# Hybrid encoder layer: modulations in steps of 256 columns with half the buffers, and S5 table products that may go to VectorE or GpSimd

## The chip, the cores and the metric

The kernel runs on one core of one Trainium2 chip, in one launch. The metric is the device time of one execution in microseconds (us). Of the kernel before three executions were timed; a fourth was profiled, and all traces here are of that one.

## What is computed

One encoder layer on x (1024 tokens by 1024 features, float32), conditioned on a vector c. Cut to what matters:

```python
mod = (silu(c) @ w_ada + b_ada).reshape(1, 3, 3, 1024)   # shift, scale, gate for three sub-layers
f1 = swiglu(modulate(x, mod[0, 0], mod[0, 1]), w_up1, w_down1)
x = layer_norm(alpha * x + (1 + mod[0, 2]) * 0.5 * f1)
tm = token_mixer(modulate(x, mod[1, 0], mod[1, 1]))      # [mLSTM heads | S5 groups], one input
x = layer_norm(alpha * x + (1 + mod[1, 2]) * tm)         # and one output projection
f2 = swiglu(modulate(x, mod[2, 0], mod[2, 1]), w_up2, w_down2)
x = layer_norm(alpha * x + (1 + mod[2, 2]) * 0.5 * f2)
```

The S5 half of the mixer is a complex diagonal recurrence over 32 groups of 64 states in two directions. Powers of its coefficients, times its input and output matrices, depend on the weights alone and can be made ahead of the tokens: the kernel calls them tables.

## The kernel before, in words

Every matrix product of tokens is done in float32 precision by splitting each operand into a rounded part and a remainder and adding three products (`mm3`, 6936 such matmuls of 128x512 in all). The splitting, two operations for each 128x512 tile, is the largest work of VectorE (DVE).

**Order of the work.** The program is straight-line code. A planner writes it: `run_jobs` goes through the matmul jobs of the main stream in a fixed order (start, first SwiGLU up, first down product, input projections, GLU, output projection in two halves, second SwiGLU), and between them `pump` takes operations out of lanes, generators such as the layer norms, the modulations and the tables (lane "bg"), the S5 mixing, the mLSTM. `Clock` keeps a planned time for each engine, with a cost for each operation, and emits an operation when its operands should be ready. `nc.any.f(...)` gives the planner the choice of VectorE or GpSimd (POOL), `nc.copy` that of ScalarE (ACT) or VectorE; `pick` takes the engine that would be done first. So every edit can move operations anywhere behind it.

**Buffers.** 99 tiles of 128x512 (`NSLOT`) are shared by all; loads of weights run ahead as far as free tiles allow. All DMAs are issued by SyncE (SP), in the order in which the planner emits them. PSUM has 8 banks.

**Modulations** (`ada`, L637 to L678). Seven of the nine modulations are made in the background during the start: for modulation j and half y (512 columns) eight tiles of `w_ada` are loaded one step ahead, 32 small matmuls against the padded vector `cpad` fill one bank, one copy takes it out, and 16 column sums per half (`fin`, `colsum`) bring it into columns.

**Tables** (`s5_gen`, L1440 to L1704). After the modulations. For each of 16 blocks two 128x320 products per table half and for each of 8 pairs of groups two 128x512 products go to GpSimd by name (`P.tensor_tensor`), each next to a VectorE product with which it is then combined; these fill the DRAM tables `Wd` and `Vd`. At the end 16 steps make the table `Ed`, each with one GpSimd product, one VectorE product, one VectorE combination and one store (L1671 to L1694).

**Who waits.** The first layer norm (`ln`) closes the first down product; the mixer's S5 part reads the tables; the output projection's second half (the passes END) needs the mLSTM of all eight chunks of tokens, each closed by `finalize` (statistics, a scaling, four transposes of 128x128, four scaled copies).

Of the kernel before, what the change touches and what calls it, by code (L numbers as in the profile page):

```python
# [11 lines left out]
OP = mybir.AluOpType  # L12
# [383 lines left out]
class Kern:  # L396
# [240 lines left out]
    def ada(self, js):  # L637


        nc = self.nc  # L640
        todo = [(j, y) for j in js for y in range(2)]

        def load(j, y):
            return [self.ada_load(j, 4 * y + x) for x in range(4)]

        nxt = load(*todo[0])
        pa = {}
        prev = None

        def fin(j, y, acc):  # L650
            for x in range(4):
                self.colsum(pa[j][:, 4 * y + x:4 * y + x + 1], acc[:, x * 128:(x + 1) * 128], self.one)
            if y:
                nc.vector.tensor_tensor(self.mods[:, j * 8:j * 8 + 8], pa[j][:, :8],
                                        self.v["b_ada"][:, j * 8:j * 8 + 8], op=OP.add)
                self.free(pa[j])

        for i, (j, y) in enumerate(todo):
            w, nxt = nxt, load(*todo[i + 1]) if i + 1 < len(todo) else None
            yield  # L660
            pb = self.bank()
            for x in range(4):
                for kc in range(KD):
                    c = slice(kc % 4 * 32, kc % 4 * 32 + 32)
                    nc.tensor.matmul(pb[c, x * 128:x * 128 + 128], self.cpad[:, kc, :], w[x][kc // 4][:, kc % 4, :],
                                     start=x == 0 and kc < 4, stop=x == 3 and kc >= 4)
            del w
            acc = self.S()
            nc.copy(acc, pb)
            yield  # L670
            if y == 0:
                pa[j] = self.bank(True)
            if prev:
                fin(*prev)
            prev = (j, y, acc)
            del acc
            yield
        fin(*prev)  # L678

    def mod(self, sub, which):  # L680
# [698 lines left out]
    def s5_gen(self):  # L1379
        nc, I = self.nc, self.I  # L1380
        V, P = nc.vector, nc.gpsimd
# [151 lines left out]
        for j in range(2, 10):  # L1533
            x, y = j // 2, j - j // 2
# [3 lines left out]
        pw = [self.S([128, G, 10]) for _ in range(2)]  # L1538
        pv_ = self.S([128, 2, G, 8])
        pv = [pv_[:, c] for c in range(2)]  # L1540
# [10 lines left out]
        for q in range(4):  # L1551
# [4 lines left out]
            br, bi_, cr, ci = (bc[:, i] for i in range(4))  # L1556
# [3 lines left out]
            cv = self.S([128, 4, 8, 16])  # L1560
            t1, t2, cv = cv[:, 2], cv[:, 3], [cv[:, c] for c in range(2)]
# [17 lines left out]
            for b4 in range(2):  # L1579
                b = 2 * q + b4  # L1580
                ws = []
                for b2_ in range(2):
                    bt = 2 * b + b2_
                    gs = slice(2 * bt, 2 * bt + 2)
                    ls_ = slice(4 * b4 + 2 * b2_, 4 * b4 + 2 * b2_ + 2)
                    w = [self.S([128, 2, 10, 16]) for _ in range(2)]
                    t1, t2 = self.S([128, 2, 10, 16]), self.S([128, 2, 10, 16])

                    def bcs(x):
                        return x[:, ls_].unsqueeze(2).to_broadcast([128, 2, 10, 16])  # L1590

                    def bcj(x):
                        return x[:, gs].unsqueeze(3).to_broadcast([128, 2, 10, 16])

                    P.tensor_tensor(t2, bcs(ci), bcj(pw[1]), op=OP.mult)
                    V.tensor_tensor(t1, bcs(cr), bcj(pw[0]), op=OP.mult)
                    yield
                    V.tensor_tensor(w[0], t1, t2, op=OP.subtract)
                    P.tensor_tensor(t2, bcs(ci), bcj(pw[0]), op=OP.mult)
                    yield  # L1600
                    V.tensor_tensor(t1, bcs(cr), bcj(pw[1]), op=OP.mult)
                    yield
                    V.scalar_tensor_tensor(w[1], t1, -1.0, t2, op0=OP.mult, op1=OP.subtract)
                    yield
                    for c in range(2):
                        nc.sync.dma_start(
                            self.Wd[b, c, :, b2_ * 256:(b2_ + 1) * 256].rearrange("p (g x) -> p g x", g=2),
                            w[c][:, :, 1:9, :].rearrange("p g j h -> p g (j h)"))
                    ws.append(w)
                    del t1, t2, w  # L1610
                    yield
                for c in range(2):
                    for gi in range(2):
                        for b2_ in range(2):
                            co = slice(32 * (2 * b4 + b2_), 32 * (2 * b4 + b2_) + 32)
                            for d in range(2):
                                l = slice(d * 64, d * 64 + 64)
                                g = 4 * b4 + 2 * b2_ + gi
                                nc.tensor.matmul(pks[d][co, :128], cz[c][l, g],
                                                 ws[b2_][c][l, gi, 2 * d:2 * d + 8].rearrange("p j h -> p (j h)"),  # L1620
                                                 start=c + gi == 0, stop=c + gi == 2)
                del ws
                yield
                gs = slice(4 * b, 4 * b + 4)
                ls_ = slice(4 * b4, 4 * b4 + 4)

                def vb(x):
                    return x[:, ls_].unsqueeze(2).to_broadcast([128, 4, 8, 16])

                def vj(x):  # L1630
                    return x[:, gs].unsqueeze(3).to_broadcast([128, 4, 8, 16])

                for c in range(2):
                    t1, t2 = self.S([128, 4, 8, 16]), self.S([128, 4, 8, 16])
                    P.tensor_tensor(t2, vb(cv[1]), vj(pv[1 - c]), op=OP.mult)
                    V.tensor_tensor(t1, vb(cv[0]), vj(pv[c]), op=OP.mult)
                    yield
                    yield
                    V.tensor_tensor(t1, t1, t2, op=OP.subtract if c == 0 else OP.add)
                    yield  # L1640
                    pt = self.bank()
                    for g in range(4):
                        nc.tensor.transpose(pt[:, g * 128:(g + 1) * 128],
                                            t1[:, g].rearrange("p j h -> p (j h)"), self.ident)
                    vt = self.S()
                    nc.scalar.activation(vt, pt, AF.Copy)
                    nc.sync.dma_start(self.Vd[b, c], vt)
                    del t1, t2, vt
                    yield
            yield  # L1650
            kc = self.S([128, 240])
# [24 lines left out]
        for b in range(8):  # L1676
            gs = slice(4 * b, 4 * b + 4)

            def A(c):
                return ea[:, c, gs].unsqueeze(3).to_broadcast([128, 4, 8, 16])  # L1680

            def B(c):
                return eb[c][:, gs].unsqueeze(2).to_broadcast([128, 4, 8, 16])

            for c in range(2):
                t1, t2 = self.S([128, 4, 8, 16]), self.S([128, 4, 8, 16])
                P.tensor_tensor(t2, A(1), B(1 - c), op=OP.mult)
                V.tensor_tensor(t1, A(0), B(c), op=OP.mult)
                yield
                yield  # L1690
                V.tensor_tensor(t1, t1, t2, op=OP.subtract if c == 0 else OP.add)
                yield
                nc.sync.dma_start(self.Ed[b, c], t1.rearrange("p g a b -> p (g a b)"))
                del t1, t2  # L1694
# [741 lines left out]
```

## Time and profile before

| | before |
|---|---|
| timed executions, us | 1943.98, 1948.27, 1949.53 (median 1948.27) |
| profiled execution, us | 1945.06 |
| its span, first to last instruction, us | 1942.9 |
| mean granted TensorE clock, share of full | 0.981 |
| PE busy, us (share of the span) | 1855.7 (96%) |
| DVE busy | 1588.7 (82%) |
| ACT busy | 650.0 (33%) |
| POOL busy | 289.5 (15%) |
| DMA, mean | 150 GB/s |

PE is TensorE, PEld its weight loads, which overlap matmuls. Matmuls are pipelined and their recorded ends modelled, so a busy PE is not one at its peak. Busy times are unions: two DVE operations that follow each other closely overlap by some hundredths of a microsecond in the records. Nearly every instruction carries the line of one helper (L79), so groups are told apart by engine, operation and shape. A tile is named by its kind: `s` one of the 99 tiles, `b` a bank, `in_...` an input.

### The profile page before, as it was taken

What the parts mean: (1) busy time and instruction counts of PE and PEld (TensorE: products, weight loads), DVE (VectorE), ACT (ScalarE), POOL (GpSimd) and SP (SyncE); (2) the same over time, 40 slices, a digit from 0 to 9 for tenths busy, and PEclk for the clock granted to TensorE, in tenths of its full rate; (3) what the DMA queues carried; (4) which work ended last, traced back from release to release, by engine and by line L of the source; (5) the groups of instructions that cost most, each with busy time, mean ns of one, the idle gap of its engine ahead of it and who ended that gap; (6) DMA issues with size and microseconds to landing.
All of it is one profiled execution on the core that took longest, in us unless ns stands there. A gap on an engine that the chain in (4) does not pass through costs nothing.

```text
span 1942.9 us, 29666 instructions
## 1 busy us (share of the span) xinstructions
PE 1855.7 (96%) x10544; PEld 1470.2 (76%) x10544; DVE 1588.7 (82%) x3267; ACT 650.0 (33%) x1190; POOL 289.5 (15%) x284
## 2 busy tenths in 40 slices
PE   5999999999999899899999899999999999999996
PEld 3677887777878677777778677678888888887775
DVE  7937889888899999879887797898677767697887
ACT  4513333333324125622243432542222222233412
POOL 0000001122100212101022421301111111100014
PEclk9999999999999999999999799999999999999998
DMA  9983233434577445575434430224233323574512
GB/s 326 361 304 137 88 129 107 136 127 133 161 276 242 155 151 194 187 214 167 149 102 129 125 105 12 76 77 136 82 113 104 109 81 109 174 259 143 183 44 76
DMA packets 187587, 290.54 MB, mean 150 GB/s; under 512 B 27280, under 2 KB 55056, under 8 KB 187440
## 3 DMA queue, kind: packets, MB, share of 16 engines
q1 hardware_dynamic: 187440, 288.65, 44.7%
q8 instruction: 83, 1.36, 0.3%
q14 instruction: 64, 0.52, 0.1%
HBM read 218.26 MB, written 70.32 MB: 149 GB/s over the span
## 4 chain that ended last, share of the span: by engine, by line
PE 76%; DVE 14%; DMA 5%; issue 3%; ACT 1%; SPq 0%; DVEq 0%; POOL 0%; ACTq 0%; POOLq 0%
PE b L79 76%; DVE s L79 13%; DMA s<-in_w_ada 1%; ACT s L79 1%; DMA s<-Wr 1%; DMA s<-in_x 1%; DVE er L79 0%; DMA s<-Vd 0%; SPq L79 0%; DMA s<-in_glu_w 0%; DMA s<-Wd 0%; DMA s<-Md 0%; DMA s<-Td 0%; DMA s<-in_w_first 0%; DVE mr L79 0%
## 5 line engine op out<-in xcount | busy, mean ns | idle before, releaser
L79 PE MATMUL b<-s 128*128 128x512 f32 (+6 forms) x9208 | 1825.6, 371 | 50.1 <-DVE s L79 34.9
L79 PEld LDWEIGHTS b<-s 128*128 128x128 f32 (+4 forms) x9208 | 1428.4, 177 | 417.5 <-DVE s L79 52.7
L79 DVE TENSOR_TENSOR s<-s 128x512 f32<-128x512 f32 (+6 forms) x1718 | 993.0, 622 | 63.7 <-ACT s L79 37.7
L79 ACT ACTIVATE s<-s 128x512 fp32r<-128x512 f32 (+2 forms) x682 | 400.9, 625 | 579.0 <-DVE s L79 379.0
L79 POOL TENSOR_TENSOR s<-s 128x512 f32<-128x512 f32 (+2 forms) x185 | 253.9, 1386 | 1190.7 <-DVE s L79 530.3
L79 DVE TENSOR_TENSOR s<-s,b 128x512 f32<-128x512 f32 (+2 forms) x332 | 209.8, 650 | 193.7 <-PE b L79 191.4
L79 ACT ACTIVATE s<-b 128x512 f32<-128x512 f32 (+2 forms) x207 | 117.4, 576 | 483.4 <-PE b L79 438.2
L79 DVE CAST s<-s 128x512 fp32r<-128x512 f32 (+1 forms) x237 | 123.2, 522 | 9.8 <-DMA s<-in_x 3.6
L79 POOL MEMSET s<- 128x4 f32 (+4 forms) x65 | 10.1, 189 | 323.5 <-DVE s L79 246.4
L79 DVE SCALAR_TENSOR_TENSOR s<-b,gcol,s 128x512 f32<-128x512 f32 x56 | 39.4, 743 | 22.1 <-PE b L79 22.1
L79 ACT ACTIVATE s<-b,vec 128x128 f32<-128x128 f32 (+3 forms) x57 | 23.6, 464 | 84.5 <-PE b L79 82.7
L79 DVE TENSOR_TENSOR_SCAN s<-s 4x128 f32<-4x128 f32 (+1 forms) x48 | 33.4, 713 | 0.4
L79 PE MATMUL b<-ident,s 128*128 128x128 f32 (+1 forms) x208 | 30.9, 278 | 0.2 <-DVE dn L79 0.2
L79 PEld LDWEIGHTS b<-ident,s 128*128 128x128 f32 (+1 forms) x208 | 24.8, 148 | 7.6 <-issue 1.9
L79 DVE SCALAR_TENSOR_TENSOR s<-s 128x320 f32<-128x320 f32 (+3 forms) x43 | 26.6, 625 | 4.4 <-ACT s L79 4.0
L79 ACT ACTIVATE s<-s,vec 128x512 f32<-128x512 f32 x26 | 19.5, 779 | 27.7 <-DVE s L79 27.7
L79 DVE SCALAR_TENSOR_TENSOR s<-s,vec 128x512 f32<-128x512 f32 (+1 forms) x36 | 26.9, 768 | 0.1
L79 ACT ACTIVATE s<-s,Bp,Gp 128x512 f32<-128x512 f32 x26 | 20.1, 805 | 18.2 <-DVE s L79 18.2
L79 ACT ACTIVATE s<-s,gcols 128x128 f32<-128x128 f32 x64 | 20.1, 393 | 5.3 <-POOL s L79 5.3
L79 PE MATMUL b<-one,s 128*32 128x1 f32 x576 | 9.4, 173 | 12.4 <-DVE s L79 12.0
L79 PEld LDWEIGHTS b<-one,s 128*32 128x32 f32 x576 | 8.4, 112 | 16.7 <-DVE s L79 12.4
L79 DVE SCALAR_TENSOR_TENSOR s<-s,gcol 128x512 f32<-128x512 f32 x24 | 18.0, 748 | 0.6
(102 smaller groups left out, 325.0 us busy)
## 6 DMA issues: line engine op xcount, KB each, us to landing
s<-in_w_up SPq DMA_DIRECT2D x170, 256.0 KB
s<-in_w_ada SPq DMA_DIRECT2D x144, 256.0 KB
Td<-s SPq DMA_DIRECT2D x140, 256.0 KB
s<-Td SPq DMA_DIRECT2D x140, 256.0 KB
s<-in_w_down SPq DMA_DIRECT2D x124, 256.0 KB
s<-in_x SPq DMA_DIRECT2D x32, 256.0 KB
Xd<-s SPq DMA_DIRECT2D x32, 256.0 KB
s<-in_w_vo SPq DMA_DIRECT2D x32, 256.0 KB
```

What stands on the lines that cost most here:

```text
L79: self.eng, self.alts, self.emit = eng, (), lambda: getattr(real, name)(*args, **kw)
```

## The change

In `ada` a step now covers 256 columns: four steps for each modulation in place of two, each with four loads in flight one step ahead in place of eight, 16 small matmuls and one copy of 128x256. Two steps share one tile `acc`, and the column sums run after every second step, as many as before. In `s5_gen` the four products that named GpSimd now go through `nc.any`: in the loops these are 32 products of 128x320 and 32 of 128x512 (16 for `Vd`, 16 for `Ed`).

```diff
-        todo = [(j, y) for j in js for y in range(2)]
+        todo = [(j, y) for j in js for y in range(4)]
 
         def load(j, y):
-            return [self.ada_load(j, 4 * y + x) for x in range(4)]
+            return [self.ada_load(j, 2 * y + x) for x in range(2)]
...
-                self.colsum(pa[j][:, 4 * y + x:4 * y + x + 1], acc[:, x * 128:(x + 1) * 128], self.one)
-            if y:
+                self.colsum(pa[j][:, 2 * y + x - 2:2 * y + x - 1], acc[:, x * 128:(x + 1) * 128], self.one)
+            if y == 3:
...
-            for x in range(4):
+            for x in range(2):
                 for kc in range(KD):
...
-            acc = self.S()
-            nc.copy(acc, pb)
+            if acc is None:
+                acc = self.S()
+            nc.copy(acc[:, y % 2 * 256:y % 2 * 256 + 256], pb[:, :256])
...
-            if prev:
-                fin(*prev)
-            prev = (j, y, acc)
-            del acc
+            if y % 2:
+                if prev:
+                    fin(*prev)
+                prev, acc = (j, y, acc), None
...
-                    P.tensor_tensor(t2, bcs(ci), bcj(pw[1]), op=OP.mult)
+                    nc.any.tensor_tensor(t2, bcs(ci), bcj(pw[1]), op=OP.mult)
...
-                    P.tensor_tensor(t2, bcs(ci), bcj(pw[0]), op=OP.mult)
+                    nc.any.tensor_tensor(t2, bcs(ci), bcj(pw[0]), op=OP.mult)
...
-                    P.tensor_tensor(t2, vb(cv[1]), vj(pv[1 - c]), op=OP.mult)
+                    nc.any.tensor_tensor(t2, vb(cv[1]), vj(pv[1 - c]), op=OP.mult)
...
-                P.tensor_tensor(t2, A(1), B(1 - c), op=OP.mult)
+                nc.any.tensor_tensor(t2, A(1), B(1 - c), op=OP.mult)
```

**Order, first place: GpSimd during the tables.** `MEMSET s 128x4x16` stands at the start of each of the four rounds of `Wd` and `Vd`; the rows of 128x320 and 128x512 between are the products. Before:

```order
L79 MEMSET s 128x4x16 x4
L79 TENSOR_TENSOR s<-s 128x320 x4
L79 TENSOR_TENSOR s<-s 128x512 x2
L79 TENSOR_TENSOR s<-s 128x320 x4
L79 TENSOR_TENSOR s<-s 128x512 x24
L79 TENSOR_SCALAR s<-s,vec 128x512 x2
```

and now:

```order
L79 MEMSET s 128x4x16 x8
L79 TENSOR_TENSOR s<-s 128x512
L79 MEMSET s 128x4x16 x8
L79 TENSOR_TENSOR s<-s 128x512 x7
L79 TENSOR_SCALAR s<-s,vec 128x512
```

No product of a table is left on GpSimd: all 32 of 128x320 and, by the counts of the whole program, 42 operations of 128x512 (32 of them the tables') have gone to VectorE.

**Order, second place: SyncE at the end of the first down product.** `s<-Td_101` is the last load of that product's left factors, `s<-in_w_f` the first weights of the mixer, `Xd<-s` the store of the first layer norm, `Ud<-s` that of the mixer's S5 input. Before:

```order
L79 DMA s<-Td_101 128x512
L79 DMA Ed<-s 128x512 x2
L79 DMA s<-in_w_f 128x512 x4
L79 DMA Ed<-s 128x512 x2
L79 DMA s<-in_w_f 128x512 x6
L79 DMA Xd<-s 128x512 x6
L79 DMA s<-in_w_f 128x512 x2
L79 DMA Xd<-s 128x512 x2
L79 DMA Ed<-s 128x512
L79 DMA Ud<-s 128x8x64
```

and now:

```order
L79 DMA s<-Td_101 128x512
L79 DMA s<-in_w_f 128x512 x6
L79 DMA Xd<-s 128x512 x6
L79 DMA s<-in_w_f 128x512 x2
L79 DMA Xd<-s 128x512
```

Nine of the sixteen stores of `Ed` stood behind `s<-Td_101` before (five here, four a few rows on); now all sixteen stand ahead of it.

**Order, third place: TensorE at the end of the mLSTM.** `b<-ident,s 128x128 x4` are the transposes of one chunk's `finalize`, `b<-s 128x512` matmuls of the main stream, `b<-s 128x129` and `b<-s 64x129` matmuls of the mLSTM. Before:

```order
L79 MATMUL b<-s 128x129 x4
L79 MATMUL b<-s 128x512 x27
L79 MATMUL b<-ident,s 128x128 x4
L79 MATMUL b<-s 128x512 x27
L79 MATMUL b<-ident,s 128x128 x4
L79 MATMUL b<-s 128x512 x9
L79 MATMUL b<-ident,s 128x128 x4
L79 MATMUL b<-s 128x512 x15
L79 MATMUL b<-ident,s 128x128 x4
L79 MATMUL b<-s 128x512 x21
L79 MATMUL b<-ident,s 128x128 x4
L79 MATMUL b<-s 128x512 x6
```

and now:

```order
L79 MATMUL b<-s 128x129 x4
L79 MATMUL b<-s 128x512 x9
L79 MATMUL b<-s 128x129 x4
L79 MATMUL b<-s 128x512 x6
L79 MATMUL b<-ident,s 128x128 x4
L79 MATMUL b<-s 128x512 x15
L79 MATMUL b<-ident,s 128x128 x24
L79 MATMUL b<-s 128x512 x132
```

The transposes of the last six chunks now follow each other with no matmul of the main stream between them, and the matmuls that stood there have moved up between those of the mLSTM.

## Rows read from the trace of the kernel before

**Rows 1.** The page, busy time of each engine and its share of the span.

```profile
PE 1855.7 (96%) x10544; PEld 1470.2 (76%) x10544; DVE 1588.7 (82%) x3267; ACT 650.0 (33%) x1190; POOL 289.5 (15%) x284
```

**Rows 2.** Stretches: busy us of each engine, granted clock, DMA share, GB/s.

```profile
50.00:100.00 50.00, 49.44 (x854) 34.24 (x853) 47.19 (x86) 26.05 (x44) 2.44 (x2) 1.00 0.99 356
302.00:537.60 235.60, 235.55 (x1210) 183.49 (x1208) 208.43 (x384) 77.89 (x140) 50.82 (x60) 1.00 0.43 139
632.50:806.00 173.50, 155.32 (x762) 122.86 (x761) 169.10 (x291) 65.13 (x109) 36.21 (x24) 0.95 0.51 169
1041.70:1222.00 180.30, 171.66 (x935) 134.62 (x934) 134.79 (x489) 66.79 (x178) 47.65 (x41) 0.92 0.29 85
```

**Rows 3.** Waits of the weight loads, 28 to 165 us.

```profile
PEld b L79 <- DMA s<-in_w_ada: 3.0, 8, 0.5
```

**Rows 4.** Groups of ScalarE by form, 17 to 302 us: copies out of a bank.

```profile
L79 ACT ACTIVATE s<-b 128x512 f32<-128x512 f32 x41 | 24.4, 598 | 98.3 <-PE b L79 98.2
```

**Rows 5.** Groups of VectorE by form, 150 to 300 us, no product on GpSimd.

```profile
L79 DVE TENSOR_TENSOR s<-s 128x512 f32<-128x512 f32 x56 | 37.2, 687 | 0.7
L79 DVE TENSOR_TENSOR s<-s 128x512 fp32r<-128x512 f32 x53 | 36.5, 689 | 10.1 <-ACT s L79 9.4
```

**Rows 6.** Groups of VectorE by form, 302 to 537.6 us.

```profile
L79 DVE TENSOR_TENSOR s<-s 128x512 f32<-128x512 f32 x101 | 73.0, 749 | 1.4
L79 DVE TENSOR_TENSOR s<-s 128x512 fp32r<-128x512 f32 x77 | 60.9, 800 | 8.0 <-ACT s L79 7.1
L79 DVE TENSOR_TENSOR s<-s,b 128x512 f32<-128x512 f32 x44 | 30.1, 684 | 16.8 <-PE b L79 16.2
L79 DVE TENSOR_TENSOR s<-s 128x320 f32<-128x320 f32 x47 | 23.7, 514 | 0.2
```

**Rows 7.** Groups of GpSimd by form, 302 to 537.6 us.

```profile
L79 POOL TENSOR_TENSOR s<-s 128x320 f32<-128x320 f32 x32 | 30.8, 967 | 160.7 <-DVE s L79 146.5 <-PE b L79 9.9 <-DMA Wd<-s 3.1
L79 POOL TENSOR_TENSOR s<-s 128x512 f32<-128x512 f32 x16 | 19.8, 1245 | 24.7 <-PE b L79 18.2 <-DVE s L79 4.0 <-DMA Td<-s 2.5
```

**Rows 8.** Groups of VectorE and GpSimd by form, 632.5 to 806 us.

```profile
L79 DVE TENSOR_TENSOR s<-s 128x512 fp32r<-128x512 f32 x100 | 70.2, 746 | 0.9 <-ACT s L79 0.3
L79 DVE TENSOR_TENSOR s<-s 128x512 f32<-128x512 f32 x74 | 52.4, 738 | 1.3 <-ACT s L79 1.1
...
L79 POOL TENSOR_TENSOR s<-s 128x512 f32<-128x512 f32 x19 | 25.5, 1355 | 84.6 <-DVE s L79 43.6 <-PE b L79 24.1 <-ACT s L79 16.8
L79 POOL TENSOR_TENSOR s<-s 128x512 fp32r<-128x512 f32 x3 | 8.4, 2803 | 28.5 <-ACT s L79 28.5
```

**Rows 9.** Waits of the weight loads, 632 to 806 us.

```profile
PEld b L79 <- DVE s L79: 20.2, 5, 8.6
```

**Rows 10.** The end of the first layer norm's wait, columns as in rows 2.

```profile
770.00:790.00 20.00, 14.03 (x51) 10.30 (x50) 19.46 (x31) 13.36 (x23) 4.29 (x4) 0.83 0.41 147
```

**Rows 11.** The DMAs that store and read the table Ed.

```profile
L79 SPq DMA_DIRECT2D Ed<-s x16: 319/320/507, 655.2 to 802.6; - x16
L79 SPq DMA_DIRECT2D s<-Ed x16: 320/387/707, 826.4 to 946.9; - x16
```

**Rows 12.** The mLSTM where no matmul of the main stream runs, columns as in rows 2.

```profile
1061.00:1118.00 57.00, 51.24 (x368) 40.07 (x366) 42.66 (x147) 26.27 (x81) 25.26 (x25) 0.79 0.42 121
```

**Rows 13.** The chain that ended last, at the end of the mLSTM (start us, us).

```profile
1162.14 24.31 issue
1186.49 1.26 POOL s L79
1187.80 12.35 PE b L79 x52
```

More of the change, by code (lines that the diff above doesn't have):

```diff
@@ L640, in ada @@
         nc = self.nc
-        todo = [(j, y) for j in js for y in range(2)]
+        todo = [(j, y) for j in js for y in range(4)]
         def load(j, y):
-            return [self.ada_load(j, 4 * y + x) for x in range(4)]
+            return [self.ada_load(j, 2 * y + x) for x in range(2)]
         nxt = load(*todo[0])
-        pa = {}
+        pa, acc = {}, None
         prev = None
@@ L665, in ada @@
                     nc.tensor.matmul(pb[c, x * 128:x * 128 + 128], self.cpad[:, kc, :], w[x][kc // 4][:, kc % 4, :],
-                                     start=x == 0 and kc < 4, stop=x == 3 and kc >= 4)
+                                     start=x == 0 and kc < 4, stop=x == 1 and kc >= 4)
             del w
-            acc = self.S()
-            nc.copy(acc, pb)
+            if acc is None:
+                acc = self.S()
+            nc.copy(acc[:, y % 2 * 256:y % 2 * 256 + 256], pb[:, :256])
             yield
```

## The prediction

> **What bounds the kernel now.** I read the page first, then the busy time of each engine by stretches of the main stream, then, where TensorE is not full, the waits and the groups by form. On the page PE is busy 96% of the span, DVE 82%, ACT 33%, POOL 15% [rows 1]. So at most 1942.9 − 1855.7 = 87 us of idle PE can be had, and only in the places where it lies. The stretches [rows 2] show where the edited code stands: at the start (50 to 100 us) PE works 49.4 of 50 us, while the DMAs are at 0.99 of their time and 356 GB/s; during the tables (302 to 537.6 us, second half of the first SwiGLU) PE works 235.55 of 235.60 us; around the first layer norm (632.5 to 806) only 155.3 of 173.5 us, with DVE at 169.1; around the mLSTM (1041.7 to 1222) 171.7 of 180.3 us at a clock of 0.92. Only the last two have time to give. In the stretch of the layer norm DVE sets the pace, and the weight loads wait 20.2 us for its tiles [rows 9].
>
> **The start.** The edit of the modulations leaves the work of PE as it was. It has half as many `w_ada` loads ahead, so ten of the first `w_up1` loads go out eight loads earlier, and the last `w_ada` load later. Eight loads of 128x512 float32 are 2.1 MB, at 356 GB/s [rows 2] 5.9 us: the most that an earlier weight could give. The other way, the weight loads waited for `w_ada` eight times, 3.0 us together [rows 3]; with half the cover I let that double, +3.0. Between −5.9 and +3.0 I take 0, since PE is full there already. The fourteen more copies out of a bank cost ACT less than 14 × 0.598 = 8.4 us [rows 4], half that for half the width, on an engine that works a third of the time: 0; without that cover they delay a column sum, not a matmul of the main stream.
>
> **Tables of 302 to 538 us.** Thirty-two products of 128x320 and sixteen of 128x512 leave POOL and come to DVE. One of 128x320 takes DVE 0.514 us [rows 6], one of 128x512 0.687 us when POOL is quiet [rows 5]: 32 × 0.514 + 16 × 0.687 = 27.4 us more work. Something comes back: with POOL's products beside them, DVE's two-input operations took 749 and 800 ns [rows 6], without them 687 and 689 [rows 5]. That is 101 × 0.062 + 77 × 0.111 = 14.8 us, so DVE has 12.6 us net to fit in. It stood idle 235.6 − 208.4 = 27.2 us there [rows 2], 16.2 of that waiting for PE [rows 6], and PE has no gap. So I take 0, with +12.6 as the upper bound if the products fall between a split and the weight load that needs it. POOL spent most of its time waiting for DVE (146.5 us [rows 7]), so a table step ends earlier when one engine does both products. The order shows this: all sixteen `Ed` stores now stand ahead of `s<-Td_101`, nine behind it before.
>
> **The first layer norm, 632 to 806 us.** Before, `Ed` steps run up to 802.6 us [rows 11], beside the layer norm, and the first reader comes at 826.4. Their early end is the gain: from 770 to 790 us DVE is busy 19.46 of 20, and PE idles 20 − 14.03 = 6.0 us at a clock of 0.83, 20 × 0.17 = 3.4 us [rows 10]. With nine steps gone I take both back: −9.4. Against that, sixteen products at 0.687 come to DVE, 11.0 us, in a stretch where it is saturated. The lengthening there is 100 × (0.746 − 0.689) + 74 × (0.738 − 0.687) = 9.5 us over 22 POOL operations [rows 5, 8]; with 16 of the 22 gone, 6.9 come back. Net +4.1, all of it on the path. Sum for the stretch −9.4 + 4.1 = −5.3. Bounds: −20.2, the whole wait [rows 9], and +11.0 if nothing comes back.
>
> **The mLSTM.** No operation is edited here, but the planner, behind a changed history, has put the main matmuls elsewhere. Before, 57 us (1061 to 1118) held no main matmul: PE idled 57 − 51.24 = 5.8 us, and at a clock of 0.79 lost 57 × 0.21 = 12.0 us [rows 12]. Now some run in between. But they are taken from the end: the transposes of the last six `finalize` follow each other with nothing between, where before the main matmuls covered them. How much they covered is seen in the chain: 24.31 us of issue before the passes END, in which PE waited for nothing [rows 13]. What is given (at most 17.8) and what is taken (at most 24.3) are the same matmuls moved, so I take 0, with −17.8 and +24.3 as ends.
>
> **Sum.** 0 + 0 − 5.3 + 0 on the profiled execution's 1945.06 gives 1939.8 us. The median of the timed runs lies 3.2 above that execution, so I name 1943.0. A measurement of this kernel can tell about 0.3%, or 5.8 us, from no change: faster is below 1942.4, slower above 1954.1. The forecast stands at that edge.
>
> **Rivals.**
> *DVE is freed altogether.* POOL's table products take 0.967, 1.245 and 1.355 us [rows 7, 8]. If DVE stands still while such a product runs, 32 × 0.967 + 16 × 1.245 + 16 × 1.355 = 72.5 us come back against 27.4 + 11.0 = 38.4 added. In the layer norm's stretch alone 21.7 − 11.0 = 10.7 are then left over, and with the 9.4 of the order the 20.2 us wait is gone: 1948.3 − 20.2 = 1928. For it speaks that DVE is saturated there; against it, the lengthening seen is 14.8 us for 48 products, 0.31 each, not 1.06.
> The Trainium skill, SBUF — State Buffer, "Who interferes with whom", states such a mechanism: the pair of ports that VectorE and GpSimd share is locked for a whole instruction, and the other fully blocks. The trace agrees that one lengthens the other, but not with the size; by that rule the time would be this rival's.
>
> *The tail of the mLSTM is exposed (the other side).* If the last six `finalize`, statistics on DVE and scalings on ACT, now run while PE has nothing else, PE waits up to 24.3 us [rows 13] just ahead of END, and its clock may drop. If the earlier mixing returns less than about 13 of the 17.8 us, this outweighs the layer norm's gain: 24.3 − 5.3 − 12 = +7 at the clock's return alone, and +19 with none of it: 1955 to 1967. For it speaks the order, against it the 12.0 us that half clock costs now.
>
> *Nothing to see.* Nothing that is needed sooner ends sooner: DVE is saturated with splits around the layer norm, the freed 9.4 us are eaten by 11.0 us of products, and the mLSTM's two changes cancel: 1948 ± 5. For it: PE is full in all the other stretches.
>
> That the products stay on GpSimd isn't open: the order shows none left there.
>
> **How the numbers follow.** Forecast 0.36 (own range 1937 to 1949), DVE freed 0.20, tail exposed 0.22, nothing to see 0.22. Half of the forecast's cases fall below 1942.4, with the second case and a little of the last: 0.41 faster; the rest of forecast and most of the last give 0.35 within 0.3%; 0.24 slower. The range goes from 1922 (the freed DVE and a start 5.9 us earlier) to 1960, the middle of the exposed tail.
>
> **What would show it.** Right: POOL busy falls by about 72 us to near 217; DVE's two-input operations at 302 to 538 us are back near 690 ns, with PE still full; the last `Ed` store ends before 775 us; PE from 770 to 790 has under 2 us idle; weight loads wait for DVE some 5 us less before 806. The mLSTM shows a clock above 0.92, and a wait of PE ahead of END, of about equal worth. Wrong: PE is no longer full at 302 to 538; the wait at the layer norm is as long as before or gone altogether; or one of the mLSTM's two changes is over 10 us larger than the other.

## The result, and the profile after

The changed kernel took 1964.82 us (median of four, 1961.15 to 1967.4) against 1948.61 for the kernel before on the same chip: a ratio of 1.0089, 95% interval 1.0074 to 1.0104. It is 16 us slower, outside the range of 1922 to 1960. The profiled execution of the kernel before (1945.06 us) was 3.6 us under that median and that of the changed kernel (1966.13) 1.3 over its own, so stretches read from the two profiles sum to about 21 us, not 16.

The page of the changed kernel, busy time of each engine; the span is 1964.4 us:

```profile
PE 1857.4 (95%) x10544; PEld 1469.8 (75%) x10544; DVE 1594.2 (81%) x3351; ACT 648.0 (33%) x1200; POOL 193.0 (10%) x204
```

The work of PE is the same as in [rows 1]; POOL lost 96 us, DVE gained 5.5. So nearly all of the loss is time in which PE idles: 1964.4 − 1857.4 = 107.0 us in place of 87.2. To find where, the starts of the same matmuls are compared: the 6936 matmuls of the main stream come in one order in every kernel here. The next table is worked out from the traces: by how many us each stretch between two of them is longer than in the profile of the kernel before (a stretch is named by the numbers of its first and last matmul).

| kernel | start 0–456 | tables 456–2280 | first layer norm 2280–2904 | S5, projections 2904–3672 | mLSTM 3672–4008 | rest | sum |
|---|---|---|---|---|---|---|---|
| changed | +1.9 | −2.3 | −5.5 | +8.3 | **+17.6** | +1.6 | 21.6 |

The spans differ by as much up to a tenth (1964.4 − 1942.9). The mLSTM alone accounts for the size of the loss; the gain at the layer norm is there and is given back in the stretch behind it. Stretches of the changed kernel (columns as in [rows 2]): the tables, the layer norm, its end, the mLSTM, its start, its tail.

```profile
302.00:540.20 238.20, 238.20 (x1253) 186.83 (x1253) 220.06 (x478) 81.84 (x149) 2.53 (x13) 1.00 0.44 144
632.00:800.00 168.00, 155.05 (x762) 122.60 (x760) 163.56 (x272) 69.04 (x117) 11.48 (x8) 0.95 0.55 191
770.00:790.00 20.00, 19.76 (x84) 15.44 (x84) 19.55 (x31) 11.74 (x21) 3.08 (x2) 1.00 0.62 203
1055.10:1229.80 174.70, 146.98 (x808) 112.67 (x805) 122.42 (x475) 62.22 (x171) 36.96 (x34) 0.88 0.29 84
1060.00:1100.00 40.00, 25.60 (x132) 19.41 (x131) 21.43 (x58) 16.77 (x49) 19.31 (x17) 0.74 0.46 127
1187.00:1204.40 17.40, 6.42 (x23) 3.46 (x21) 15.80 (x98) 7.70 (x26) 0.00 (x0) 0.60 0.01 1
```

The mLSTM of the kernel before between the same two matmuls:

```profile
1052.80:1210.00 157.20, 148.56 (x838) 116.26 (x837) 120.94 (x469) 58.41 (x156) 43.60 (x38) 0.91 0.28 83
```

PE does the same work, but idles 174.7 − 147.0 = 27.7 us in place of 8.6. Two places hold most of it: 14.4 us from 1060 to 1100, and 11.0 us from 1187 to 1204, where DVE works through the bare `finalize` of the last six chunks at 15.8 of 17.4 us. The clock is down in the same two places, at 0.74 and 0.60. What ends the first is in the chain of the changed kernel, 1055 to 1206 us (start us, us, what), and in the waits of DVE and POOL of 1055 to 1230 us (us in total, times, longest):

```profile
1068.87 14.75 DMA s<-Wr
...
1138.40 12.57 DMA s<-Wr
```

```profile
DVE s L79 <- DMA s<-Wr: 16.6, 4, 6.1
...
POOL s L79 <- DMA s<-Wr: 15.1, 1, 15.1
```

Only the wait at the start costs PE time. During the second one, from 1138 to 1151 us, PE is busy 13.00 of 13.00 us.

In the kernel before, the same loads were no faster: the last of the first four stands in the chain for 16.18 us, and while it is under way the DMA engines move 50 GB/s (last two columns). But DVE hardly waited (1052 to 1210 us):

```profile
1058.67 16.18 DMA s<-Wr
```

```profile
1055.00:1060.00 5.00, 5.00 (x24) 4.03 (x22) 0.73 (x2) 0.00 (x0) 0.00 (x0) 1.00 0.13 50
```

```profile
DVE s L79 <- DMA s<-Wr: 0.6, 1, 0.6
```

`s<-Wr` is the load in `direction` that puts a row of decay factors on 64 partitions each for two heads (L2215): two of 128x512 for each direction at its second and its fifth chunk, eight in all, each followed by a multiplication. The kernel before issued all eight between 1050.7 and 1088.0 us, ahead of their use; the changed kernel from 1058.9 to 1138.4, each pair just before it. The planner counts on 2 us for any load to land.

VectorE of the changed kernel by form, 302 to 540.2 us, answers to [rows 6]:

```profile
L79 DVE TENSOR_TENSOR s<-s 128x512 f32<-128x512 f32 x121 | 81.1, 696 | 1.2
L79 DVE TENSOR_TENSOR s<-s 128x512 fp32r<-128x512 f32 x78 | 53.0, 689 | 6.2 <-ACT s L79 4.3 <-PE b L79 1.2
L79 DVE TENSOR_TENSOR s<-s 128x320 f32<-128x320 f32 x80 | 37.1, 485 | 0.0
```

The waits of the weight loads for DVE, 632 to 800 us, and the stores of `Ed`, which answer to [rows 9] and [rows 11]:

```profile
PEld b L79 <- DVE s L79: 13.4, 3, 8.1
```

```profile
L79 SPq DMA_DIRECT2D Ed<-s x16: 319/320/327, 628.1 to 742.9; - x16
```

### The profile page after: what moved, and what is told of

Its sections match the earlier page's. It is cut to its first block, busy times and chain, and to the rows that moved or that the text cites. A ratio compares the mean times of both kernels' runs of the same rounds, so it can differ in the third digit from the quotient of the medians.

```text
span 1964.4 us, 29686 instructions
## 1 busy us (share of the span) xinstructions
PE 1857.4 (95%) x10544; PEld 1469.8 (75%) x10544; DVE 1594.2 (81%) x3351; ACT 648.0 (33%) x1200; POOL 193.0 (10%) x204
## 4 chain that ended last, share of the span: by engine, by line
PE 76%; DVE 13%; DMA 6%; issue 2%; ACT 2%; SPq 1%; POOL 0%; DVEq 0%; ACTq 0%
PE b L79 76%; DVE s L79 11%; ACT s L79 2%; DMA s<-Wr 1%; DMA s<-in_w_ada 1%; DMA s<-Vd 1%; DMA s<-in_x 1%; SPq L79 1%; DVE er L79 0%; DVE mr L79 0%; DMA Ud<-s 0%; DMA s<-Yd 0%; DVE st L79 0%; DMA s<-Ed 0%; DMA s<-in_w_first 0%
## 5 line engine op out<-in xcount | busy, mean ns | idle before, releaser
L79 DVE TENSOR_TENSOR s<-s 128x512 fp32r<-128x512 f32 (+5 forms) x1792 | 1003.5, 606 | 82.5 <-ACT s L79 28.3
L79 ACT ACTIVATE s<-s 128x512 fp32r<-128x512 f32 (+3 forms) x674 | 395.9, 625 | 580.6 <-DVE s L79 388.0
L79 DVE TENSOR_TENSOR s<-s,b 128x512 f32<-128x512 f32 (+1 forms) x332 | 210.2, 651 | 185.9 <-PE b L79 185.2
L79 ACT ACTIVATE s<-b 128x512 f32<-128x512 f32 (+3 forms) x219 | 119.5, 553 | 493.1 <-PE b L79 456.5
L79 POOL TENSOR_TENSOR s<-s 128x512 f32<-128x512 f32 (+1 forms) x111 | 160.1, 1458 | 1184.3 <-DVE s L79 441.8
L79 DVE SCALAR_TENSOR_TENSOR s<-s 128x320 f32<-128x320 f32 (+3 forms) x43 | 22.5, 529 | 4.7 <-ACT s L79 4.4
L79 PEld LDWEIGHTS b<-one,s 128*32 128x32 f32 x576 | 8.4, 112 | 15.8 <-DVE s L79 12.6
```

The costliest lines, as they stand in the source:

```text
L79: self.eng, self.alts, self.emit = eng, (), lambda: getattr(real, name)(*args, **kw)
```

## The experiments

Three theories stood at the outset. O: the loss is the order in which the planner writes the mLSTM, which any edit upstream may flip. P: it is the products on VectorE. S: it is the start, with half the buffers of `w_ada`. Later ones are named where they come up. Each group of runs was timed beside the kernel before, whose medians there lie between 1946.7 and 1948.9 us; the ratios are to those. The differences by stretch, in us against the profile of the kernel before:

| run | edit | median, us | start | tables | layer norm | S5 | mLSTM | rest |
|---|---|---|---|---|---|---|---|---|
| e1 | modulations alone | 1954.2 | +3.5 | −1.4 | +3.8 | +4.3 | −2.9 | +1.1 |
| e2 | products alone | 1956.3 | +0.9 | −1.1 | −7.9 | −1.0 | +16.5 | +1.3 |
| e3 | before, new mLSTM order | 1970.0 | +3.3 | +8.8 | −6.7 | +3.5 | +17.0 | +1.4 |
| e4 | products of `Ed` alone | 1985.0 | −0.2 | 0.0 | +1.7 | +4.1 | +31.5 | +0.9 |
| e5 | all edits, old mLSTM order | 1961.4 | +5.9 | −6.6 | +8.7 | +6.8 | −2.6 | +0.7 |
| e6 | changed, plain loads for `Wr` | 1952.3 | +0.4 | −2.4 | −5.5 | +5.6 | +3.1 | +0.3 |
| e7 | changed, convolutions first | 1992.3 | +5.5 | −2.4 | −5.2 | +102.1 | −50.6 | +0.5 |
| e8 | before, convolutions first | 2002.3 | +1.3 | 0.0 | +1.3 | +104.5 | −54.2 | +1.1 |
| e9 | changed, 64 copies of `Wr` | 2023.2 | +3.0 | −2.4 | −5.6 | +77.2 | +2.0 | +1.4 |
| e10 | products alone, 64 copies | 2011.3 | −1.9 | −1.1 | −8.9 | +71.1 | +5.1 | +1.6 |
| e11 | before, 64 copies | 2021.1 | +2.8 | 0.0 | +0.6 | +72.1 | −0.6 | +3.4 |
| e12 | changed, two steps of `w_ada` ahead | 1964.1 | +0.8 | −0.6 | −6.1 | +8.8 | +16.7 | +0.9 |
| e13 | changed, 8 copies of `Wr` | 1953.1 | +3.0 | −2.4 | −5.2 | +8.4 | +4.4 | +1.4 |
| e14 | products alone, 8 copies | 1947.3 | +4.7 | −1.1 | −8.0 | +2.8 | +4.1 | +0.3 |
| e15 | before, 8 copies | 1949.3 | +1.0 | 0.0 | 0.0 | −1.0 | −0.4 | +1.4 |
| e16 | as e14, `Mr` by chunk | 1946.3 | +2.9 | −1.1 | −8.0 | +5.3 | +6.2 | +1.6 |
| e17 | changed, `Wr` in two halves | 1951.5 | +3.9 | −2.4 | −5.5 | +6.8 | +3.4 | +1.5 |
| e18 | products alone, two halves | 1943.9 | +0.6 | −1.0 | −9.0 | −0.2 | +4.0 | −0.2 |

Single profiles scatter. In the start, nine runs (e2, e4, e8, e10, e11, e14, e15, e16, e18) have the same order on every engine as the kernel before, and show −1.9 to +4.7; behind the layer norm, in the S5 stretch, e2, e14, e16 and e18 share one order on TensorE and show −1.0 to +5.3. In the mLSTM the four runs with the changed order and the loads as they were (changed, e2, e3, e12) agree within 1.1.

### Each half of the change, and its order without the change

e1 takes the edits of `ada` alone, e2 the four of `s5_gen` alone, e4 of these only the last. e3 has none of them, and in the planner's table of lanes:

```diff
-"bg": (3.5, 6)}
+"bg": (3.5, 5)}
```

> Only the modulations in steps of 256 columns; the table products stay on GpSimd. The planner then writes the mLSTM (from matmul 3300 of the main stream on) in the very order of the kernel before. Theory O (the 17 us come from the order in which the planner writes the mLSTM, which any upstream edit may flip): 1948 within 4 us. Theory P (they come from the products that VectorE now carries): 1948 as well. Theory S (half the buffers of w_ada): about 1962 to 1966.

> Only the S5 table products on either engine; the modulations as before. The mLSTM comes out in the order of the changed kernel. Theory O: 1965 within 4 us, with the mixer's second half (from the first matmul of the output projection on) as in the changed kernel. Theory P: 1965 too. Theory S: 1948.

> The kernel before with none of the change's edits: all table products on GpSimd, modulations in steps of 512. One number of the planner is moved (the background lane leaves 5 tiles free, not 6), and the mLSTM comes out in the order of the changed kernel, the same sequence on TensorE, VectorE and SyncE from matmul 3300 on. Theory O: slower by 15 to 22 us, 1963 to 1970, all of it between matmuls 3672 and 4008. Theory P and theory S: 1948 within 4 us.

> Only the sixteen products of the table Ed on either engine. The planner writes a third order of the mLSTM: all eight finalize at its end (32 transposes in a row) and the second pair of Wr loads of both directions only behind matmul 3875. Theory O: slower than the kernel before by at least the 17 us of the changed kernel, 1965 to 1985, though only 16 of 64 products moved. Theory P: a quarter of 17 us, about 1952.

Measured: ratios to the kernel before of 1.004 (1.0027 to 1.0053) for e1, 1.0041 (1.0024 to 1.0058) for e2, 1.0115 (1.009 to 1.0139) for e3, 1.0192 (1.0175 to 1.0209) for e4. Three stretches of the mLSTM (e2, e3, e4, from matmul 3672 to 4008), and e3's products on GpSimd at 302 to 545 us, where they still are:

```profile
1043.50:1217.20 173.70, 146.56 (x820) 112.54 (x809) 122.64 (x475) 62.14 (x171) 37.00 (x34) 0.89 0.28 84
```

```profile
1061.00:1235.20 174.20, 148.18 (x818) 114.08 (x808) 122.46 (x475) 62.19 (x171) 37.03 (x34) 0.88 0.28 84
```

```profile
1057.90:1246.60 188.70, 145.18 (x811) 111.94 (x806) 123.57 (x481) 59.63 (x159) 46.41 (x44) 0.86 0.25 77
```

```profile
L79 POOL TENSOR_TENSOR s<-s 128x320 f32<-128x320 f32 x32 | 35.0, 1097 | 116.8 <-DVE s L79 108.6 <-PE b L79 8.2
```

In the stretch of the mLSTM theory O holds without exception: e2 and e3, with the order of the changed kernel, lose 16.5 and 17.0 us whether the products are on VectorE or not; e1, with the order of before, loses nothing; e4, with a third order, loses 31.5 though it moves 16 products of 64 (how its loss divides between the later loads and a longer bare end was not tried). P and S fall for this stretch. But O's totals for e1 and e2 missed: e1 loses 6 us more than forecast, in the start, the layer norm and the S5 stretch; e2 comes out 9 us better, with 7.9 of gain at the layer norm and no loss behind it; what it has ahead of the changed kernel lies mostly there, in the S5 stretch (−1.0 in place of +8.3).

In e4 the chain of 1057 to 1230 us shows the same loads, later still:

```profile
1072.23 19.27 DMA s<-Wr
...
1154.59 19.29 DMA s<-Wr
```

### All edits in the old order; plain loads; the convolutions' lane first

e5 moves one number (`"bg": (3.5, 10)`). e6 reads weights where the row stood:

```diff
-nc.sync.dma_start(x, self.bc_ap(self.Wr, (d * 4 + 2 * a) * S + hc * 512,
-                                [[S, 2], [0, 64], [1, 512]]))
+nc.sync.dma_start(x, self.I["w_out"][128 * a:128 * a + 128, 512 * (hc % 2):512 * (hc % 2) + 512])
```

In e7 and e8 the entry `"conv": (2.5, 6)` of the table of lanes moves from behind `glu` to behind `gate`.

> All edits of the change, all 64 products on VectorE, and one number of the planner moved (the background lane leaves 10 tiles free, not 6): the mLSTM comes out in the order of the kernel before, the same sequence on TensorE, VectorE and SyncE from matmul 3300 on; the tables end later (last store of Ed near matmul 3007). Theory O (the order of the mLSTM costs the 17 us): from matmul 3672 to 4008 it takes 157 us within 4, as before, and the whole is 1946 to 1956. Theory P (the products on VectorE cost it): 1962 or more.

> The changed kernel, its order on TensorE, VectorE and SyncE unchanged, but the eight broadcasts of Wr into tiles are replaced by loads of as many bytes from rows of w_out (so the mLSTM is scaled by other numbers). Theory W (the broadcasts land 12 to 15 us after their issue, and VectorE, in order, stands behind them; that is what the new order exposes): the waits of 14.75 and 12.57 us go, 1940 to 1953. Theory Q (they wait in the queue behind the loads issued ahead of them): a plain load waits as long, within 4 us of the changed kernel's 1965. Theory F (only the bare transposes of the last finalize cost): 1960 to 1966.

> All edits of the change; the lane of the convolutions stands ahead of the S5 lanes in the planner's list, not behind them, so the mLSTM may start at matmul 3432, not 3684: the Wr loads go out well ahead of their use and the transposes of finalize end by matmul 3783. Theory O: the loss of the mLSTM goes and part of what the kernel before lost there too: 1930 to 1948. Rival: the S5 mix is delayed by as much, the GLU waits, and the sum stays at 1955 to 1970.

> The kernel before, with the convolutions' lane ahead of the S5 lanes and none of the change's edits: the control to the run above. Theory O: 1930 to 1946, faster than before by what the half clock and the idle time of its mLSTM cost at most (18 us). Theory P: at least 10 us faster than the run above, since its products stay on GpSimd; theory O: within 8 us of it.

e5: 1.007 (1.0048 to 1.0091). The mLSTM is back at 154.6 us with all products on VectorE, as O has it. The total missed: the tables now end late (the background lane holds fewer tiles), and layer norm and S5 lose 15.5.

e6 leaves out the decay factors, so its result is not the layer's; its loads and its order are what is compared. It is at 1.0014 (0.9999 to 1.0028), 12.5 us below the changed kernel's median, with TensorE and VectorE in the same order. The mLSTM of e6 from matmul 3672 to 4008, and its start:

```profile
1050.60:1210.90 160.30, 142.97 (x813) 109.53 (x805) 122.92 (x475) 62.01 (x171) 36.84 (x34) 0.94 0.31 92
1055.00:1095.00 40.00, 36.12 (x222) 27.14 (x221) 31.06 (x87) 24.46 (x73) 23.91 (x22) 0.96 0.67 182
```

PE is busy for 36 of 40 us where the changed kernel had 25.6, at a clock of 0.96 in place of 0.74, and 14.5 of the 17.6 us are gone. Theory W holds, Q (the queue) falls: loads of the same size in the same place land in time. F, the bare tail, is the 3.1 us that stay: PE still waits at the end, but the matmuls that covered that end before now stand further ahead.

e7 and e8 missed widely: 1.0228 (1.0208 to 1.0247) and 1.0279 (1.0259 to 1.03). The mLSTM went ahead, and the stretch ahead of it grew by twice what its own shrank by. Two stretches of e7, from 1042 to 1105 and from 1153 to 1260 us:

```profile
1042.40:1104.60 62.20, 49.69 (x244) 39.14 (x243) 26.04 (x66) 24.46 (x49) 10.33 (x9) 0.86 0.47 129
...
1153.10:1259.70 106.60, 91.11 (x420) 71.39 (x419) 79.23 (x293) 36.16 (x83) 10.85 (x9) 0.90 0.21 67
```

PE idles 12.5 and 15.5 us and its clock falls to 0.86 and 0.90. That the mLSTM's small matmuls had too few of the main stream between them is the likely reason; it was not tried. The two kernels end 10 us apart, e7, with the products on VectorE, ahead: where the products run isn't what this loss hangs on.

### Why the loads land late: copies, halves

Theory A: the 64 partitions that read one row make the load slow. e9 (changed), e10 (products alone) and e11 (before) keep 64 copies of `Wr`, e13 to e15 keep 8:

```diff
-self.Wr = dr.tile([2, 4, S], F32, name="Wr")
+self.Wr = dr.tile([2, 4, 8, S], F32, name="Wr")
...
-[[S, 2], [0, 64], [1, 512]]))
+[[S, 16], [0, 8], [1, 512]]))
```

The store repeats its row as often, and the planner's cost of it is divided by the copies, so that the order on TensorE stays. e16 is e14 with `Mr` laid out by chunk, so that a partition of its broadcasts reads `[[0, 128], [1, 512]]`, not `[[0, 128], [S, 4], [1, 128]]`. e12 loads two steps of `w_ada` ahead in the changed kernel.

> The changed kernel with Wr kept 64 times in DRAM, so that each of the 64 partitions of a broadcast reads a copy of its own; same result, same order on TensorE, and 2 MB more to store near matmul 3250. Theory A (64 partitions that read one row of 2 KB make the load slow): it lands like a plain load, and the time comes near that of the run with plain loads, 1949 to 1957. Theory R (something else in these loads, the wait on the table's store or their place in the queue): 1961 to 1968.

> Products on either engine, modulations as before, Wr kept 64 times. Theory A: 12 us less than the run with the products alone (1956.3), 1941 to 1949, about the kernel before or a little faster. Theory R: 1953 to 1960.

> The control: the kernel before with Wr kept 64 times. Its order issues these loads early enough (0.6 us of waits for them), so theory A and theory R both give 1948 within 4 us; the 2 MB more of stores may cost up to 6.

> The changed kernel with two steps of w_ada ahead, as many buffers as before; same order from matmul 2904 on. Theory O: the start gives back at most the 1.8 us that the changed kernel loses by matmul 456, so 1961 to 1967. Theory S (half the buffers): 1945 to 1955.

> The changed kernel with 8 copies of Wr, each read by 8 partitions; same result and order. Theory A with a store that costs by its copies (64 cost about 73 us, so 8 about 9 or less): the loads land early enough, the mLSTM from matmul 3672 to 4008 takes 158 to 165 us (174.7 in the changed kernel), the whole 1950 to 1962. Theory R: 1965 or more.

> Products on either engine alone, with 8 copies of Wr: the run with the products alone (1956.3) less 10 to 16 us in the mLSTM, plus up to 9 for the stores: 1940 to 1955. At the lower end it beats both kernels.

> The control: the kernel before with 8 copies of Wr. It has no wait to lose, so what it is slower by (0 to 9 us, 1948 to 1957) is the price of the copies alone.

> As the products alone with 8 copies of Wr, and the rows of Mr laid out by chunk, so that a partition of its sixteen broadcasts reads 2 KB in a piece and not four times 512 bytes. If these loads also hold the mLSTM's start: 3 to 8 us below the run without this edit; if not, within 4 us of it.

e9, e10 and e11 came to 2023.2, 2011.3 and 2021.1 us: all missed, by the stores. They add 71 to 77 us to the S5 stretch of each; in e9 (930 to 1050 us) ScalarE waits for them:

```profile
ACT s L79 <- DMA Wr<-s: 74.6, 1, 74.6
```

Inside the mLSTM, though, e9 differs from the kernel before by only +2.0, e10 by +5.1. With 8 copies the stores cost nothing that shows: e15 is at 1.0005 (0.9995 to 1.0016). e13 is at 1.0022 (1.0007 to 1.0038), 11.8 us below the changed kernel, e14 at 0.9989 (0.9974 to 1.0003). DVE of e13 from 1055 to 1220 us:

```profile
DVE s L79 <- DMA s<-Wr: 3.3, 1, 3.3
```

e16 (1946.3 us, 0.9995, interval 0.9984 to 1.0006) is within a microsecond of e14, so the broadcasts of `Mr` hold nothing that shows. e12 is at 1.0076 (1.0059 to 1.0093): twice the buffers give nothing back, and S falls.

But the copies had changed two things: how many partitions read a row, and the first dimension of the load's source (2 before, 128 with 64 copies, 16 with 8). What the DMA engines did while DVE waited in the changed kernel points to the second; the last two columns are their busy share and GB/s:

```profile
1072.00:1076.00 4.00, 0.00 (x0) 0.00 (x0) 0.69 (x1) 0.00 (x0) 0.00 (x0) 0.78 0.13 50
1076.00:1080.00 4.00, 0.33 (x2) 0.33 (x3) 2.28 (x4) 0.00 (x0) 0.00 (x0) 0.50 0.21 73
...
1138.00:1142.00 4.00, 4.00 (x19) 3.23 (x18) 0.00 (x0) 0.42 (x1) 0.00 (x0) 1.00 0.10 38
```

0.13 of 16 engines are 2.1, so about two engines, and at 50 GB/s a pair of 256 KB takes 10.5 us by estimate. The Trainium skill, DMA: Bandwidth & Descriptors, "Why a DMA increments its semaphore by 16 and not by 1", says that a copy is spread over the largest number of engines, up to 16, that divides the first dimension, leaving out those of size 1, of both its patterns; for a source of 2 that is two, and the trace agrees with 0.13 of 16. e17 (changed) and e18 (products alone) change only that dimension, with one copy and the same row:

```diff
-nc.sync.dma_start(x, self.bc_ap(self.Wr, (d * 4 + 2 * a) * S + hc * 512,
-                                [[S, 2], [0, 64], [1, 512]]))
+for p in range(2):
+    nc.sync.dma_start(x[p * 64:p * 64 + 64], self.bc_ap(self.Wr, (d * 4 + 2 * a + p) * S + hc * 512,
+                                                        [[0, 64], [1, 512]]))
```

> The changed kernel, one copy of Wr as there, but each of its eight loads issued as two of 64 partitions, whose source pattern begins with a dimension of 64 in place of one of 2; same bytes from the same row, same order on TensorE. Theory E (a load whose source begins with a dimension of 2 is carried by 2 of the 16 DMA engines: 0.13 of their time is busy, at 50 GB/s, while VectorE waits): the waits of 14.75 and 12.57 us fall below 5, the mLSTM takes 158 to 163 us, the whole 1949 to 1956. Theory A (64 partitions that read one row): nothing changes, 1962 to 1968.

> The products on either engine alone, with the same two halves for each load of Wr. Theory E: 1941 to 1948, as with 8 copies (1947.3) or a little less, since there are no copies to store; theory A: 1953 to 1960.

e17: 1951.52 us, 1.0015 (1.0003 to 1.0027). e18: 1943.92 us, 0.9979 (0.9968 to 0.999), 0.2% faster than the kernel before. The stretch of e17 that answers to the first row above, its start of the mLSTM, and DVE's wait:

```profile
1072.00:1076.00 4.00, 2.77 (x22) 1.74 (x18) 4.00 (x13) 1.25 (x5) 2.21 (x2) 1.00 0.44 84
1060.00:1100.00 40.00, 35.70 (x227) 26.79 (x228) 32.02 (x92) 24.68 (x74) 25.45 (x23) 1.00 0.76 178
```

```profile
DVE s L79 <- DMA s<-Wr: 3.1, 1, 3.1
```

Theory E holds and A falls: 64 partitions still read one row, and the loads land in time. That the loads are now twice as many and half as large isn't what does it: in e13 they are as many and as large as in the changed kernel, begin with a dimension of 16, and land in time too. From 1060 to 1100 us the clock is 1.00 where the changed kernel had 0.74. The time comes back in one place: from matmul 3708 to 3720, where the first four loads are waited for, the changed kernel takes 28.5 us, e6, e13 and e17 14.0 to 14.4.

## Why the prediction was wrong

**The mLSTM: this step failed.** It took what the moved matmuls give at the start and take at the end as alike, hence 0, with ends of −17.8 and +24.3. Cut at matmul 3900, ahead of the bare transposes, the end takes 18.2 us more than before; all that stands ahead of it gives back 0.6 in the changed kernel, but 14.9 in e17, where the loads land in time. So the balance comes near with such loads (+3.1, +4.4 and +3.4 in e6, e13, e17). What the step lacked is that the new order also issues the loads of `Wr` just before their use, and that they land late: the gain at the start, forecast as at most 17.8, all but failed to come, and the stretch costs 17.6 us. The prediction names no load of the mLSTM and reads the order there on PE's side alone; SyncE's order, where the eight loads stand, would have shown them later, and the profile of before that they move at 50 GB/s. [rows 12] hid it, since before the loads had been issued ahead.

The upper end was also read from the wrong engine. The 24.31 us of issue in [rows 13] are GpSimd's: it stood idle for 24.3 us before its operation at 1186.5. PE was busy over that time (35.81 of the 37 us from 1150 to 1187), so the row says nothing of the length of the bare tail, and that 18.2 lies under it is luck.

**The rival on the other side** had the place (PE bare ahead of END, 11 us idle at a clock of 0.60) and its own condition right: the earlier mixing returns less than 13 us, namely 0.6. It doesn't say why that should be; the loads are that reason. Its 1955 to 1967 held the time. The forecast's sign of being wrong, one of the mLSTM's two changes over 10 us larger than the other, came true; the clock of the stretch fell from 0.91 to 0.88 where above 0.92 had been the sign of being right.

**The tables, 302 to 538 us: right.** Forecast 0, measured +0.8 up to the end of that stretch. DVE's operations fell to 696 and 689 ns, as in [rows 5], its busy time rose by about 10 us between the same two matmuls (11.6 in the rows shown, which are 2.6 us apart in length) where 12.6 had been worked out, and PE stayed full: 238.20 of 238.20. POOL's busy time fell by 96 us on the page, not by 72: ten more operations of 128x512 left it than the table's products. A product of 128x320 took 0.485, not 0.514 us.

**The rival of a freed DVE: wrong.** DVE's work grew there instead of shrinking. DVE did not stand still for the length of POOL's products: taking POOL's products away gave back the 0.05 to 0.11 us per operation that [rows 6] had shown over [rows 5].

**The first layer norm: right, in sum and by its terms.** Forecast −5.3, measured −5.5: the matmuls that stood from 770 to 790 us take 9.1 us less (−9.4), the rest of the stretch 3.7 more (+4.1). The last store of `Ed` is issued at 742.9 us, PE idles 0.24 us from 770 to 790, and the weight loads wait 13.4 us for DVE, not 20.2. The gain is that of the early `Ed`: over the kernels the stretch follows the issue of its last store, whoever multiplies.

| kernel | e2 | e3 | changed | e4 | before | e1 | e5 |
|---|---|---|---|---|---|---|---|
| last store of `Ed` issued, us | 699.2 | 713.9 | 742.9 | 801.9 | 802.6 | 808.5 | 843.3 |
| layer norm, us | −7.9 | −6.7 | −5.5 | +1.7 | 0 | +3.8 | +8.7 |

e3, whose products stay on GpSimd, loses 8.8 us in the stretch of the tables besides; the changed kernel and e2 lose nothing there.

**The start: right.** Forecast 0 between −5.9 and +3.0, measured +1.9, within the −1.9 to +4.7 of equal programs.

**A stretch that was not costed: S5, matmuls 2904 to 3672, +8.3.** The layer norm's gain is lost here. The weight loads wait 10.3 us for DVE from 800 to 1055 us, 5.6 before, 3.7 in e2. Of the 8.3 us, 3.7 are lost by matmul 3000, right behind the layer norm, where the weight loads wait 4.2 us for DVE (812 to 832 us); e12, e13, e17 and e6, with both halves too, lose 3.6 to 5.2 there, e2, e14, e16 and e18 nothing. The rest comes and goes between kernels with one order: all kernels here with both halves of the change lose 5.6 to 8.8 (leaving out e7 and e9, whose loss there has another cause, as e10's has), those with the products alone −1.0 to +5.3. The modulations alone (e1) lose 4.3 with every engine in the order of before from matmul 2904 on, and e3 and e4, with no edit of the modulations, 3.5 and 4.1. So both halves together cost most here, but neither an edit nor an order explains it all, and the cause stays open.

**The numbers.** The predicted 1943.0 lacked 17.6 for the mLSTM and 8.3 for S5; with them it would have been 1968.9, against 1964.8 measured. The 4 us too many are of the size by which the two profiled executions lie apart from their medians.

## What to carry to other kernels

Where a planner writes the order, an edit can cost nothing where it stands and 17 us two thousand matmuls further on; so compare the order of every queue, SyncE's too, at each place where it differs, and look for loads that used to be early. Changing one planner number in the kernel before (e3) tells an edit's own cost from that of a flipped order. And look at the first dimension of a load's source: here one that began with 2 was better issued as two loads that begin with 64 partitions, and this gave 12 to 13 us.

## What was not expected of the hardware

A load of 256 KB whose source begins with a dimension of 2 kept 0.13 of the 16 DMA engines busy at 50 GB/s, and the wait for a pair of them stood 14.75 us in the chain; halved by partitions the same bytes left VectorE a wait of 3.1 us. While PE stood still there, the granted clock fell to 0.78 (1072 to 1076 us) and then to 0.50 (1076 to 1080), the lower of its two levels. Stores that repeat 4 rows 64 times held ScalarE for 74.6 us, with the DMA engines at 0.23 and 31 GB/s from 960 to 980 us; those that repeat them 8 times for nothing that shows; why the price isn't in proportion was not tried.
